# Chunk pairs in the 16-to-32 step of a triangular inverse, and the diagonal blocks of the decay table copied by ScalarE instead of VectorE

## Chip, core and metric

The kernel runs on one core of one Trainium2 chip. The time is device microseconds (us) of that core, the median of several executions. The core's engines each run their own queue in order: TensorE (PE; its weight loads are shown apart as PEld), VectorE (DVE), ScalarE (ACT), GpSimd (POOL), and SyncE (SP), which here issues the DMAs.

## What is computed

One decoder layer on 2048 tokens of width 1024: an input projection; a gated DeltaNet with 8 heads (chunked linear attention); a memory attention with 4 heads beside it; an output projection; layer norm; a squared-ReLU MLP of width 4096; layer norm. All inputs are float32. The part that the change touches is the chunked delta rule. For each chunk of tokens and each head it needs the solution of a unit lower triangular system:

```python
lower = jnp.where(strict, jnp.einsum('bnhcd,bnhsd->bnhcs', k_beta, kc) * decay, 0.0)
a_mat = jnp.eye(CHUNK, dtype=f32) + lower
u = lax.linalg.triangular_solve(a_mat, v_beta, left_side=True, lower=True, unit_diagonal=True)
w = lax.linalg.triangular_solve(a_mat, k_beta * jnp.exp(gc)[..., None], left_side=True,
                                lower=True, unit_diagonal=True)
```

The kernel takes chunks of 128 tokens and forms the inverse of the unit triangular matrix itself, once for each head and chunk.

## The kernel before

**Blocks and stages.** The 2048 tokens go in 4 blocks of 512 (`NB`), a block is 4 chunks of 128 (`NC`). In each block the 8 heads pass through `dense` (the projections aq, ak, av, az, each 24 matmuls with 512 columns, a convolution and a gate), `gdn_a` (key products pkq, the decayed table dl, its inverse by `invert`), and one head later `gdn_b` (the recurrence over the state: products pc and po). Then come the output projection (ao) and the MLP (af). Large products are split into a high and a low fp32r part, so three matmuls make one; the small ones of `invert` and `gdn_b` are plain float32, and the profile counts two passes (a weight load and a matmul each) for one such product.

**The inverse.** `invert` (L803) gets the table L (dl) of a head: 128 rows by 4 chunks by 128 columns. There are 32 inverses in a run, 8 heads by 4 blocks, and each handles 4 chunks at once. It works from small diagonal blocks to large ones:

- The diagonal blocks of 32 rows are copied out of L into Lq, a quad of 32 partitions at a time, with VectorE (L808), and their left halves into LB with GpSimd (L809). From Lq two VectorE instructions pick the 16-row blocks (Lc), and a loop of 15 steps with three VectorE instructions each inverts those 16-row blocks (Xc).
- The step from 16 to 32 rows: Z holds the 16-row inverses at their places, ZT is its transpose by VectorE. XB gets the blocks of Z on its diagonal (ScalarE, four copies, L843). TensorE multiplies LB with the lower half of ZT, one product of 16 columns for each chunk (pq, L849); ScalarE copies the result to Q (L850); TensorE multiplies XB with Q, again one product for each chunk (pp, L853); VectorE subtracts that from ZT (L854). The products use 112 of 128 stationary columns.
- The steps from 32 to 64 (L875 to L891) and from 64 to 128 rows (L893 to L904) have the same shape, but there two chunks share one product: L32, X32, X64 and LP have room for 2 chunk pairs, and a pair occupies different rows and columns. These products are pq and pp with 32 and with 64 columns.

**What sets the order of the work.** All instructions are recorded first. `Recorder.issue` then puts each engine's instructions in one fixed order with a list schedule: it goes by cost formulas for each operation (`Recorder.cost`), latencies between engines (`LAT`, `LAT_FROM`, a margin of 100 ns), and the place in the program as priority. The schedule of the whole kernel is made in one go, so a changed operation in `invert` can move instructions anywhere behind it. TensorE gets the products of `invert`, with matmuls of the projections of other heads between a product and the product that needs its result. Every instruction is issued from one line, so the profile shows L400 for all, and the tile names tell them apart.

Of the kernel before, what the change touches and what calls it, by code (L numbers as in the profile page):

```python
# [10 lines left out]
AF = mybir.ActivationFunctionType  # L11
ALU = mybir.AluOpType
AX = mybir.AxisListType

P = 128
TB = 512
NC = TB // P
# [399 lines left out]
def hybrid_layer(  # L417
# [24 lines left out]
    nc = tc.nc  # L442
# [21 lines left out]
    def small(name, shape, bufs=3, dt=F32):  # L464
        return rec.buf(sm, shape, dt, name, bufs, name)

    def bank(name, tag):
        return rec.buf(ps, (P, TB), F32, tag, PBUFS[tag], name)
# [12 lines left out]
    half = cst.tile([P, 2], F32, name="half")  # L481
# [20 lines left out]
    nc = rec  # L502
# [6 lines left out]
    NI = 1  # L509
    inv = []  # L510
    for i in range(NI):
        d = {}
        for n, shape in (("XB", (NC, P)), ("LB", (NC, P)), ("L32", (2, P)), ("X32", (2, P)), ("X64", (2, P)),
                         ("LP", (2, P)), ("Q", (2 * P,))):
            d[n] = rec.buf(cst, (P,) + shape, F32, n + str(i), 1, n)
            nc.gpsimd.memset(d[n], 0.0)
        inv.append(d)
# [285 lines left out]
    def invert(L, par):  # L803

        Lq = small("Lq", [P, 32, NC], 2)
        for q in range(4):
            r = slice(32 * q, 32 * q + 32)
            nc.vector.tensor_copy(Lq[r].rearrange("p f c -> p c f"), L[r, :, 32 * q:32 * q + 32])  # L808
            nc.gpsimd.tensor_copy(inv[par % NI]["LB"][r, :, 32 * q:32 * q + 16], L[r, :, 32 * q:32 * q + 16])  # L809
        L32, LP = inv[par % NI]["L32"], inv[par % NI]["LP"]  # L810
        for p in range(2):
            rows = slice(64 * p + 32, 64 * p + 64)
# [8 lines left out]
                                       op0=ALU.mult, op1=ALU.add)  # L821
        Xc = small("Xc", [P, 16, NC], 2)
        nc.vector.tensor_copy(Xc, i16.unsqueeze(2).to_broadcast([P, 16, NC]))
        B = small("Bc", [P, 16, NC], 2)
        for j in range(15):
# [3 lines left out]
                                    in1=Lc[:, j:j + 1].to_broadcast([P, w, NC]), op=ALU.mult)  # L829
            nc.vector.tensor_tensor(out=Xc[:, :w], in0=Xc[:, :w], in1=B[:, :w], op=ALU.subtract)  # L830
        Z = small("Z32", [P, NC, 32], 2)
        for hf in range(2):
            nc.vector.tensor_scalar_mul(Z[:, :, 16 * hf:16 * hf + 16], Xc.rearrange("p f c -> p c f"),
                                        half[:, hf:hf + 1])
        ZT = small("ZT32", [P, NC, 32], 2)
        nc.vector.transpose(ZT.rearrange("p c f -> p (c f)"), Z.rearrange("p c f -> p (c f)"))
        XB, LB, X32, X64, Q = (inv[par % NI][n] for n in ("XB", "LB", "X32", "X64", "Q"))
# [1 line left out]
        Y3 = v4(Y)  # L839
        nc.gpsimd.memset(Y, 0.0)  # L840
        quads = [slice(32 * q, 32 * q + 32) for q in range(4)]
        for r in quads:
            nc.scalar.copy(out=XB[r, :, r], in_=Z[r])  # L843

        W = P - 16
        Q16 = Q[:W, :64].rearrange("p (c f) -> p c f", c=NC).part(0)
        pq = bank("pq", "ga%d" % par)[:W, :64].rearrange("p (c f) -> p c f", c=NC)
        for c in range(NC):
            nc.tensor.matmul(pq[:, c], LB[:, c, :W], ZT[:, c, 16:32], start=True, stop=True)  # L849
        nc.scalar.copy(out=Q16, in_=pq)  # L850
        pp = bank("pp", "ga%d" % par)[:W, :64].rearrange("p (c f) -> p c f", c=NC)
        for c in range(NC):
            nc.tensor.matmul(pp[:, c], XB[:, c, :W], Q[:, c * 16:(c + 1) * 16].part(0), start=True, stop=True)  # L853
        nc.vector.tensor_tensor(out=ZT[:W, :, 16:32], in0=ZT[:W, :, 16:32], in1=pp, op=ALU.subtract)  # L854


        ZP = Lq.rearrange("p f c -> p (f c)")[:, :64].rearrange("p (c f) -> p c f", c=2)
        Z = small("Z32", [P, NC, 32], 2)
        for p in range(2):
            odd = slice(64 * p + 32, 64 * p + 64)  # L860
            nc.vector.tensor_copy(ZP[64 * p:64 * p + 32].part(2 * p + 1), ZT[odd, 2:4])
            nc.scalar.copy(out=ZP[odd].part(2 * p), in_=ZT[odd, 0:2])
        nc.vector.transpose(Z.rearrange("p c f -> p (c f)"), ZT.rearrange("p c f -> p (c f)"))
        for p in range(2):
            for u, eng in ((0, nc.gpsimd), (1, nc.vector)):
                q = quads[2 * p + u]
                eng.tensor_copy(X32[q, :, q].part((u, p)), Z[64 * p:64 * p + 32, 2 * u:2 * u + 2])
        for p in range(2):
            for u, eng in ((0, nc.gpsimd), (1, nc.vector)):
                q = quads[2 * u + p]  # L870
# [4 lines left out]
        pq = bank("pq", "ga%d" % par)[:, :64].rearrange("p (c f) -> p c f", c=2)  # L875
# [4 lines left out]
        pp = pb.rearrange("p (c f) -> p c f", c=2)  # L880
# [15 lines left out]
        pq = bank("pq", "ga%d" % par)[:, :P].rearrange("p (c f) -> p c f", c=2)  # L896
# [3 lines left out]
        pp = bank("pp", "ga%d" % par)[:, :P].rearrange("p (c f) -> p c f", c=2)  # L900
# [14 lines left out]
    def gdn_a(h, r, G):  # L915
# [29 lines left out]
        for c0 in range(0, NC, 2):  # L945
# [4 lines left out]
            for c in (c0, c0 + 1):  # L950
                nc.vector.scalar_tensor_tensor(out=dl3[:, c], in0=pkq[:, c - c0, 0], scalar=bh[:, c:c + 1], in1=dl3[:, c],
                                               op0=ALU.mult, op1=ALU.mult)
            nc.vector.tensor_tensor(out=at3[:, c0:c0 + 2], in0=pkq[:, :, 1], in1=at3[:, c0:c0 + 2], op=ALU.mult)
        Y3 = invert(dl3, par)

        pv = trans(v3, "ptv")
# [254 lines left out]
    for b in range(NB):  # L1211
# [14 lines left out]
        r, A = {}, {}  # L1226
# [142 lines left out]
```

## Time and profile before

| what | value |
|---|---|
| median of 3 runs | 2923.58 us (2921.82 to 2924.61) |
| the profiled execution | 2920.42 us |
| its span, first to last instruction | 2918.7 us |
| TensorE busy | 2876.1 us (99%), clock 0.998 |
| VectorE busy | 2181.5 us (75%) |
| ScalarE busy | 1560.7 us (53%) |
| GpSimd busy | 406.1 us (14%) |

The profile is one execution. A row of the timeline gives the start of an instruction or a merged group, its duration, engine, line, operation, output and inputs by tile name, shape, and count; a bracket tells how long the engine was idle before it and what ended that. Matmuls overlap their neighbours, so the time that a matmul takes from TensorE is read from the distance between starts and not from its duration. A row of the groups by line gives busy time, mean duration in ns, idle time before and what ended it.

### The profile page before, as it was taken

Reading aid. Unit: us, or ns where it says so; the run is one execution under the profiler, and the core shown is the slowest. Engines: PE = TensorE matmul, PEld = TensorE weight load, DVE = VectorE, ACT = ScalarE, POOL = GpSimd, SP = SyncE. Lnnn points to the kernel's source line nnn. Section 1 sums busy time; section 2 is a strip of 40 time slices with the busy share of each in tenths; the row PEclk is TensorE's granted clock in tenths of the full one; section 3 lists DMA queues with packets and bytes.
Section 4 is the critical chain, followed back from the end, with each engine's and each line's share of the span. In section 5 each row is a group of like instructions: output and inputs, shape, how many; then the busy total and the mean of one; then the engine's idle time right before and its main releaser. Section 6 shows DMA issues by size and latency. Waiting matters only on the chain.

```text
span 2918.7 us, 43334 instructions
## 1 busy us (share of the span) xinstructions
PE 2876.1 (99%) x14660; PEld 2407.3 (82%) x14660; DVE 2181.5 (75%) x5792; ACT 1560.7 (53%) x3774; POOL 406.1 (14%) x1029
## 2 busy tenths in 40 slices
PE   8999999999999999999999999999999999999998
PEld 6888778888788888888888888888888888888886
DVE  7998987666788886666678887756667888676667
ACT  6677635444366663555446665344454667444443
POOL 2233101000132211000022321100002222010000
PEclk9999999999999999999999999999999999999999
DMA  7655567555743322444473332244447332324444
GB/s 282 245 202 199 185 225 242 189 193 185 277 156 130 127 87 80 159 141 136 150 273 141 132 116 99 87 151 145 148 165 257 137 139 86 103 94 150 147 145 137
DMA packets 127710, 469.83 MB, mean 161 GB/s; under 512 B 14464, under 2 KB 16896, under 8 KB 109056
## 3 DMA queue, kind: packets, MB, share of 16 engines
q1 hardware_dynamic: 126912, 467.00, 46.9%
q8 instruction: 116, 1.90, 0.3%
q14 instruction: 106, 0.87, 0.1%
q10 hardware_dynamic: 576, 0.06, 0.0%
HBM read 402.97 MB, written 64.03 MB: 160 GB/s over the span
## 4 chain that ended last, share of the span: by engine, by line
PE 88%; DVE 6%; ACT 3%; DMA 1%; POOL 1%; issue 1%; POOLq 0%; SPq 0%; DVEq 0%; ACTq 0%
PE af L400 43%; PE ao L400 8%; PE aq L400 6%; PE az L400 5%; PE av L400 5%; PE ak L400 5%; PE amq L400 3%; PE pc L400 3%; PE pq L400 2%; PE po L400 1%; DVE y L400 1%; PE pkq L400 1%; PE pp L400 1%; PE pmo L400 1%; PE sps L400 1%
## 5 line engine op out<-in xcount | busy, mean ns | idle before, releaser
L400 DVE TENSOR_TENSOR whl<-wraw,whl 128x1024 fp32r<-128x1024 f32 (+1 forms) x446 | 541.6, 1218 | 414.6 <-ACT whl L400 412.9
L400 PE MATMUL af<-Thi,whl 128*128 128x512 f32 (+1 forms) x2304 | 649.1, 366 | 6.4 <-DVE whl L400 6.4
L400 ACT CAST whl<-wraw 128x1024 fp32r<-128x1024 f32 (+1 forms) x446 | 467.2, 1047 | 345.0 <-PE af L400 241.2
L400 PEld LDWEIGHTS af<-Thi,whl 128*128 128x128 f32 x2304 | 416.2, 189 | 77.5 <-DVE whl L400 7.3
L400 PE MATMUL af<-whl,xh 128*128 128x512 f32 x1536 | 472.1, 390 | 0.5 <-ACT whl L400 0.4
L400 PE MATMUL af<-Tlo,whl 128*128 128x512 f32 (+1 forms) x1152 | 421.3, 366 | 0.0
L400 PE MATMUL af<-whl,xl 128*128 128x512 f32 x896 | 345.5, 389 | 0.0
L400 PEld LDWEIGHTS af<-whl,xh 128*128 128x128 f32 x1536 | 287.9, 188 | 62.9 <-DVE whl L400 1.5
L400 PE MATMUL ao<-whl,ch 128*128 128x512 f32 x768 | 252.4, 402 | 0.3 <-DVE y L400 0.2
L400 PEld LDWEIGHTS af<-Tlo,whl 128*128 128x128 f32 x1152 | 217.2, 189 | 34.7
L400 POOL TENSOR_SCALAR ve<-mv 128x1 f32<-128x1 f32 x34 | 25.8, 760 | 1466.0 <-DVE mv L400 1439.0
L400 ACT ACTIVATE rl<-af 128x512 f32<-128x512 f32 x128 | 76.5, 597 | 274.4 <-PE af L400 272.6
L400 PEld LDWEIGHTS af<-whl,xl 128*128 128x128 f32 x896 | 168.2, 188 | 35.1
L400 PE MATMUL aq<-Thi,whl 128*128 128x512 f32 x512 | 181.9, 413 | 7.0 <-ACT Thi L400 7.0
L400 PE MATMUL av<-Thi,whl 128*128 128x512 f32 x512 | 178.3, 406 | 0.1
L400 PE MATMUL ak<-Thi,whl 128*128 128x512 f32 x512 | 174.0, 400 | 0.0
L400 DVE SCALAR_TENSOR_TENSOR y<-y,af 128x512 f32<-128x512 f32 x224 | 146.5, 680 | 35.4 <-PE af L400 35.4
L400 PE MATMUL az<-Thi,whl 128*128 128x512 f32 x512 | 171.3, 399 | 1.5 <-DVE whl L400 1.5
L400 PEld LDWEIGHTS ao<-whl,ch 128*128 128x128 f32 x768 | 141.6, 188 | 27.1 <-DVE y L400 0.9
L400 PE MATMUL ao<-whl,cl 128*128 128x512 f32 x384 | 154.2, 404 | 0.0
L400 PEld LDWEIGHTS aq<-Thi,whl 128*128 128x128 f32 x512 | 95.4, 192 | 21.8 <-ACT Thi L400 7.0
L400 PEld LDWEIGHTS az<-Thi,whl 128*128 128x128 f32 x512 | 95.0, 188 | 18.7 <-DVE whl L400 1.9
(256 smaller groups left out, 5839.6 us busy)
## 6 DMA issues: line engine op xcount, KB each, us to landing
wraw<-in_w_ff_dram SPq DMA_DIRECT2D x224, 512.0 KB, 4.2
whl<-wsc SPq DMA_DIRECT2D x108, 1024.0 KB, 4.8
wraw<-tsc SPq DMA_DIRECT2D x128, 512.0 KB, 3.3
wsc<-whl SPq DMA_DIRECT2D x36, 1024.0 KB, 6.0
wraw<-in_w_out_dram SPq DMA_DIRECT2D x48, 512.0 KB, 3.7
wraw<-in_w_in_dram SPq DMA_DIRECT2D x35, 512.0 KB, 7.0
wq<-in_w_ff_dram SPq DMA_DIRECT2D x64, 256.0 KB, 4.3
tsc<-wq SPq DMA_DIRECT2D x64, 256.0 KB, 3.3
```

The source lines that it names most:

```text
L400: o.fn(*[res(a) for a in o.args], **{k: res(v) for k, v in o.kw.items()})
```

## The change

In the step from 16 to 32 rows, two chunks (c and c + 2) now share one product. LB holds two chunks side by side in each 32-row block, so it is (2, 128) in place of (4, 128), and so is XB. The product of LB with the halves of ZT of both chunks gives for every row both the wanted 16 columns and those of the other chunk; two ScalarE activations copy it to Q, each with a per-partition scale (`half`, 1 on one 16-row half of each quad and 0 on the other), which makes the unwanted part zero. XB has to hold the 16-row inverses of two chunks on its diagonal: a VectorE shuffle (Xr) exchanges the 16-row halves of chunks 2 and 3, and a VectorE multiply-add (Xp) merges them with chunks 0 and 1. The four ScalarE copies to XB take half as many elements. Both products are now made 2 times with 32 columns in place of 4 times with 16, and the first one has 128 stationary columns in place of 112. Apart from that, the four copies of the diagonal blocks into Lq go from VectorE to ScalarE.

```diff
-        for n, shape in (("XB", (NC, P)), ("LB", (NC, P)), ("L32", (2, P)), ("X32", (2, P)), ("X64", (2, P)),
+        for n, shape in (("XB", (2, P)), ("LB", (2, P)), ("L32", (2, P)), ("X32", (2, P)), ("X64", (2, P)),
...
-            nc.vector.tensor_copy(Lq[r].rearrange("p f c -> p c f"), L[r, :, 32 * q:32 * q + 32])
-            nc.gpsimd.tensor_copy(inv[par % NI]["LB"][r, :, 32 * q:32 * q + 16], L[r, :, 32 * q:32 * q + 16])
+            nc.scalar.copy(out=Lq[r].rearrange("p f c -> p c f"), in_=L[r, :, 32 * q:32 * q + 32])
+            nc.gpsimd.tensor_copy(inv[par % NI]["LB"][r, :, r].rearrange("p u (k f) -> p u k f", k=2),
+                                  L[r, :, 32 * q:32 * q + 16].rearrange("p (k u) f -> p u k f", k=2))
...
+        Xr = small("Xr", [P, 16, 2], 1)
+        nc.vector.stream_shuffle(Xr, Xc[:, :, 2:4], list(range(16, 32)) + list(range(16)))
+        Xp = small("Xp", [P, 2, 16], 1)
+        nc.vector.scalar_tensor_tensor(out=Xp, in0=Xr.rearrange("p f c -> p c f"), scalar=half[:, 1:2],
+                                       in1=Z[:, 0:2, 0:16], op0=ALU.mult, op1=ALU.add)
...
-        for r in quads:
-            nc.scalar.copy(out=XB[r, :, r], in_=Z[r])
+        for q, r in enumerate(quads):
+            nc.scalar.copy(out=XB[r, :, 32 * q:32 * q + 16], in_=Xp[r])
+        pq = bank("pq", "ga%d" % par)[:, :64].rearrange("p (u f) -> p u f", u=2)
+        for c in range(2):
+            nc.tensor.matmul(pq[:, c], LB[:, c], ZT[:, c:NC:2, 16:32], start=True, stop=True)
+        Q16 = Q[:, :64].rearrange("p (u f) -> p u f", u=2)
+        nc.scalar.activation(Q16[:, :, 0:16].part(0), pq[:, :, 0:16], AF.Copy, scale=half[:, 0:1])
+        nc.scalar.activation(Q16[:, :, 16:32].part(3), pq[:, :, 16:32], AF.Copy, scale=half[:, 1:2])
         W = P - 16
-        Q16 = Q[:W, :64].rearrange("p (c f) -> p c f", c=NC).part(0)
-        pq = bank("pq", "ga%d" % par)[:W, :64].rearrange("p (c f) -> p c f", c=NC)
-        for c in range(NC):
-            nc.tensor.matmul(pq[:, c], LB[:, c, :W], ZT[:, c, 16:32], start=True, stop=True)
-        nc.scalar.copy(out=Q16, in_=pq)
-        pp = bank("pp", "ga%d" % par)[:W, :64].rearrange("p (c f) -> p c f", c=NC)
-        for c in range(NC):
-            nc.tensor.matmul(pp[:, c], XB[:, c, :W], Q[:, c * 16:(c + 1) * 16].part(0), start=True, stop=True)
-        nc.vector.tensor_tensor(out=ZT[:W, :, 16:32], in0=ZT[:W, :, 16:32], in1=pp, op=ALU.subtract)
+        pp = bank("pp", "ga%d" % par)[:W, :64]
+        for c in range(2):
+            nc.tensor.matmul(pp[:, c * 32:(c + 1) * 32], XB[:, c, :W], Q[:, c * 32:(c + 1) * 32].part(0, 3),
+                             start=True, stop=True)
+        zt = ZT[:W].rearrange("p (k u) f -> p u k f", k=2)[:, :, :, 16:32]
+        nc.vector.tensor_tensor(out=zt, in0=zt, in1=pp.rearrange("p (u k f) -> p u k f", u=2, k=2), op=ALU.subtract)
```

Because the whole schedule is made anew, the order changes in many places. Three of them follow; a row is line, operation, output and inputs by tile name, shape of the streamed operand or the result, and count.

On TensorE, the first inverse of block 0, with the key projection (ak) of another head around it. Before:

```order
L400 MATMUL pq<-ZT_1239,LB 112x16 x4
L400 MATMUL pkq<-kq 128x256 x6
L400 MATMUL pp<-Q,XB 112x16 x4
L400 MATMUL ak<-Thi,whl 128x512 x2
L400 MATMUL ak<-Tlo,whl 128x512
L400 MATMUL ak<-Thi,whl 128x512 x2
```

And now:

```order
L400 MATMUL pq<-ZT_1242,LB 128x32 x2
L400 MATMUL ak<-Thi,whl 128x512
L400 MATMUL pkq<-kq 128x256 x6
L400 MATMUL pp<-Q,XB 112x32 x2
L400 MATMUL ak<-Thi,whl 128x512
L400 MATMUL ak<-Tlo,whl 128x512
L400 MATMUL ak<-Thi,whl 128x512 x2
```

Each product of the step stands 2 times in place of 4, and between the two products there is one ak matmul more.

On TensorE, the last inverse of block 1 (the 16th of the run), its step from 64 to 128 rows, beside the output projection (ao) and the transposes of the memory attention (pmT). Before:

```order
L400 MATMUL pq<-YP,LP 128x64 x2
L400 MATMUL ao<-whl,cl 128x512
L400 MATMUL pmT<-ident,pr 128x128 x2
L400 MATMUL ao<-whl,ch 128x512 x2
L400 MATMUL ao<-whl,cl 128x512
L400 MATMUL pmT<-ident,pr 128x128
L400 MATMUL pp<-Q,X_150 128x64 x2
```

And now:

```order
L400 MATMUL ao<-whl,cl 128x512
L400 MATMUL ao<-whl,ch 128x512 x2
L400 MATMUL ao<-whl,cl 128x512
L400 MATMUL pq<-YP,LP 128x64 x2
L400 MATMUL pp<-Q,X_149 128x64 x2
L400 MATMUL ao<-whl,ch 128x512 x2
```

The product pp, which needs the ScalarE copy of pq, now follows pq directly; in the last inverses of blocks 2 and 3 it is the same.

On ScalarE, the first inverse of block 0, from the copies to XB on. Before:

```order
L400 COPY XB<-Z_1226 32x4x32 x4
L400 COPY Q<-pq 112x64
L400 COPY Lq<-ZT_1239 32x64 x2
L400 COPY Y<-ZT_1239 32x4x32 x4
L400 COPY Q<-pq 128x64
L400 COPY raw<-ak 128x512
```

And now:

```order
L400 COPY XB<-Xp 32x2x16 x4
L400 ACTIVATE Q<-pq,half 128x2x16 x2
L400 COPY Lq<-ZT_1242 32x64 x2
L400 COPY Y<-ZT_1242 32x4x32 x4
L400 COPY Q<-pq 128x64
L400 COPY Lq<-dl 32x4x32 x4
L400 ACTIVATE Y<-pp 32x2x32 x2
```

Two activations stand where one copy to Q stood, and the four Lq copies of the next head's inverse have come in between the copy of pq to Q and the instructions that read pp; the copy out of the bank of ak (raw) has moved behind them.

## The prediction

> **What bounds the kernel now.** I read the page first: busy times by engine, and the chain of work that ended last.
>
> ```profile
> span 2918.7 us, 43334 instructions
> PE 2876.1 (99%) x14660; PEld 2407.3 (82%) x14660; DVE 2181.5 (75%) x5792; ACT 1560.7 (53%) x3774; POOL 406.1 (14%) x1029
> PE 88%; DVE 6%; ACT 3%; DMA 1%; POOL 1%; issue 1%; POOLq 0%; SPq 0%; DVEq 0%; ACTq 0%
> ```
>
> TensorE works in 2876.1 of 2918.7 us, so all its idle time is 42.6 us, and 88% of the last chain is its own. The changed work lies in the stages of the heads, so I cut those out next: first the heads of block 0, then those of blocks 1 to 3, in windows of 292 us (columns: PE, PEld, DVE, ACT, POOL busy, clock, DMA share, GB/s).
>
> ```profile
> 73.00:365.00 292.00, 286.51 (x1612) 240.64 (x1610) 268.28 (x1005) 203.38 (x634) 87.55 (x209) 1.00 0.57 208
> ```
>
> ```profile
> 803.00:1095.00 292.00, 290.13 (x1650) 245.16 (x1649) 242.19 (x994) 185.37 (x635) 72.44 (x219) 1.00 0.35 125
> 1533.00:1825.00 292.00, 290.13 (x1651) 245.19 (x1651) 239.89 (x974) 181.35 (x627) 68.91 (x208) 1.00 0.34 121
> 2263.00:2555.00 292.00, 290.38 (x1645) 245.14 (x1644) 234.94 (x917) 178.41 (x604) 61.42 (x180) 1.00 0.33 115
> ```
>
> In these stages too TensorE is the limit: it idles 5.5 us in block 0 and 1.9, 1.9 and 1.6 us in the others. VectorE has 24 us left in block 0 and about 50 us elsewhere, ScalarE 89 us and more. So the time should follow the work of TensorE as long as the others deliver in time. The last view is the timeline of TensorE at the first inverse:
>
> ```profile
> 103.03 0.87 PE L400 MATMUL pq<-ZT,LB 128*112 128x16 f32 x8
> 103.75 0.96 PE L400 MATMUL pkq<-kq 128*128 128x256 f32 x6
> 104.55 0.86 PE L400 MATMUL pp<-Q,XB 128*112 128x16 f32 x8
> 105.26 0.70 PE L400 MATMUL ak<-Thi,whl 128*128 128x512 f32 x2
> 105.80 0.40 PE L400 MATMUL ak<-Tlo,whl 128*128 128x512 f32 x1
> ...
> 107.41 0.53 PE L400 MATMUL pq<-Lq,L 128*128 128x32 f32 x4
> 107.77 0.48 PE L400 MATMUL ak<-Thi,whl 128*128 128x512 f32 x1
> 108.09 0.39 PE L400 MATMUL av<-Thi,whl 128*128 128x512 f32 x1
> 108.32 0.40 PE L400 MATMUL av<-Tlo,whl 128*128 128x512 f32 x1
> 108.55 0.40 PE L400 MATMUL av<-Thi,whl 128*128 128x512 f32 x1
> ```
>
> A matmul of 512 columns in a stream takes 0.23 us from start to start (108.09, 108.32, 108.55). The eight passes of pp start at 104.55 and the next matmul at 105.26, so 0.71 us; but the two ak behind them take 0.54 us where two such take 0.45. The group therefore costs 0.71 + 0.09 = 0.80 us, 0.100 for each pass. The four passes of pq with Lq and L, whose form is that of the changed product (128 stationary columns, 32 streamed), cost 0.36 + (0.32 - 0.23) = 0.45 us, 0.113 each.
>
> **The change part by part. TensorE.** The first product has 0.72 us to the next start, and the pkq behind it takes 0.80 us where 0.72 is usual:
>
> ```profile
> 807.40 0.88 PE L400 MATMUL pkq<-kq 128*128 128x256 f32 x6
> 808.12 0.40 PE L400 MATMUL av<-Thi,whl 128*128 128x512 f32 x1
> ```
>
> So it also costs 0.80 us, and the step 1.60 us in each inverse. Now pq has four passes of a form that is in the trace, 0.45 us. The four passes of pp keep 112 stationary columns and stream 32 in place of 16: no row shows that form. Its lower bound is 4 x 0.100 = 0.40 us, its upper bound the 0.45 of the 128-column form. I take 0.40, since streamed columns do not seem to count below 128, as the products of the recurrence show:
>
> ```profile
> 814.95 0.38 PE L400 MATMUL pc<-state,ck 128*128 128x128 f32 x2
> 815.16 0.39 PE L400 MATMUL po<-state,qd 128*128 128x128 f32 x2
> 815.31 0.48 PE L400 MATMUL aq<-Thi,whl 128*128 128x512 f32 x1
> 815.62 0.40 PE L400 MATMUL aq<-Tlo,whl 128*128 128x512 f32 x1
> ```
>
> Four passes with 128 streamed columns take 0.36 + (0.31 - 0.23) = 0.44 us, no more than the four with 32. The step is then 0.85 us (up to 0.90), and an inverse saves 0.75 us (at least 0.70). All 32 inverses lie in stages where TensorE is the limit: 32 x 0.75 = 24.0 us, at least 22.4.
>
> [...]
>
> **ScalarE and VectorE.** The rows of the groups by line that carry the costs (busy us, mean ns, idle before):
>
> ```profile
> L400 DVE COPY Lq<-dl 32x128 f32<-32x128 f32 x128 | 35.0, 274 | 2.0
> L400 DVE STREAM_SHUFFLE Bc<-Xc 128x32 f32<-128x32 f32 x32 | 6.0, 187 | 0.2
> L400 DVE SCALAR_TENSOR_TENSOR gp<-gp,gz 128x32 f32<-128x32 f32 x28 | 5.1, 183 | 0.0
> L400 DVE SCALAR_TENSOR_TENSOR Lc<-Lq,half,Lc 128x64 f32<-128x64 f32 x32 | 8.9, 277 | 0.2
> ```
>
> ```profile
> L400 ACT COPY XB<-Z 32x128 f32<-32x128 f32 x128 | 37.8, 295 | 15.1 <-DVE Z L400 13.8
> L400 ACT COPY Lq<-ZT 32x64 f32<-32x64 f32 x64 | 15.5, 243 | 21.5 <-DVE ZT L400 20.8
> L400 ACT ACTIVATE vb<-ptv,vbs 128x128 f32<-128x128 f32 x128 | 36.7, 367 | 11.6 <-PE ptv L400 11.6
> L400 ACT COPY vt<-pc 128x128 f32<-128x128 f32 x128 | 34.4, 269 | 88.1 <-PE pc L400 87.1
> L400 ACT COPY Q<-pq 112x64 f32<-112x64 f32 x32 | 6.6, 208 | 8.5 <-PE pq L400 8.1
> ```
>
> For each inverse VectorE loses 4 copies of 274 ns (1.10 us) and gains a shuffle (187 ns) and a multiply-add over 32 elements, which lies between 183 and 277 ns; I take 230. That is 0.68 us less, 5.4 us in a block of 8 heads.
>
> ScalarE gains four Lq copies. Their form is that of the XB copies, 295 ns, so 1.18 us. The four XB copies shrink from 128 to 32 elements: from 295 at 128 and 243 at 64, I estimate 217 at 32, 0.31 us less. The copy to Q (208 ns) becomes two activations with a per-partition scale. Such a scale costs about 98 ns (367 against 269), and 32 elements in place of 64 save about 28 (from 269 at 128 and 208 at 64), so 0.28 us each and 0.35 us more. ScalarE has 1.22 us more for each inverse, 9.8 us in a block: 70 to 73% in block 0, 62 to 66% elsewhere. Neither engine becomes the limit, and both sums lie beside TensorE's work. What hides them is the stream of projection matmuls; without it each inverse would pay the 1.22 us.
>
> The four LB copies of GpSimd keep their number and their elements, in three dimensions: no row shows that, but GpSimd is at 21 to 30% in these stages, and by the code the copies can be made a whole loop of VectorE ahead of their product. The shuffle and the multiply-add lengthen the way from Xc to pp by up to 0.42 us, the waits for ScalarE's Lq that from dl to Lc by a few tenths; other heads' matmuls cover both, as far as the new order provides.
>
> **New waits.** A product that reads Q has to wait for ScalarE. How long, this place shows, where TensorE did wait:
>
> ```profile
> 2512.66 0.55 PE L400 MATMUL pq<-YP,LP 128*128 128x64 f32 x4
> 2513.02 0.47 PE L400 MATMUL ao<-whl,cl 128*128 128x512 f32 x1
> 2513.24 0.27 ACT L400 COPY Q<-pq 128x128 f32<-128x128 f32 x1 [0.92 <-PE pq L400]
> 2513.65 0.63 PE L400 MATMUL pp<-Q,X 128*128 128x64 f32 x4 [0.16 <-ACT Q L400]
> ```
>
> From the slot behind pq (2513.02) it takes 0.22 us to ScalarE's start, 0.27 for the copy, 0.14 to pp: 0.63 us. With two activations it is 0.22 + 0.56 + 0.14 = 0.92 us. The new order puts one ak and six pkq between pq and pp at the first inverse, 0.23 + 0.72 = 0.95 us, and counted over all 32 inverses nowhere less. So that wait should just be covered. The second place in the order is not covered: in the last inverses of blocks 1 to 3, pp follows pq at once and TensorE idles 0.63 us, 1.9 us in all.
>
> **The sum.** The profiled execution is 2920.42 us: 2920.4 - 24.0 + 1.9 = 2898.3. The median of the runs lies 3.2 us above that execution, and I expect the same of the changed kernel: 2901.5 us.
>
> **Rivals.** First, the new order eats part of the gain. The order was made from cost formulas, and the ScalarE copies come into the way of others at places like the third one, where four of them (1.18 us) stand between Q and the readers of pp. If the idle time of the four stages doubles (5.5 + 1.9 + 1.9 + 1.6 = 10.9 us), the saving is 24.0 - 1.9 - 10.9 = 11.2 us, so 2912.4. For it speaks block 0, where VectorE has only 24 us left; against it the relief of VectorE there.
>
> Second, slower: ScalarE holds up TensorE. The Lq copies wait in ScalarE's queue for dl, and behind them stand the copies out of the PSUM banks that TensorE needs back. If the four copies' 1.18 us fell on TensorE in every inverse, the loss would be 37.8 us against 24.0 gained, so 2937.4; from 0.75 us for each inverse it turns the result. Against it: ScalarE idles a third of these stages, and TensorE waits for it little now, as the list of waits shows (total us, times, longest):
>
> ```profile
> PE pq L400 <- DVE YP L400: 2.4, 10, 0.5
> PE pc L400 <- ACT vt L400: 1.8, 5, 0.5
> ```
>
> Third, no difference: a pass costs by what it streams, and the step streams 16 passes x 16 = 8 x 32 = 256 columns before and after. Then nothing is saved but the 1.9 us of new waits are paid, 2925.5. The rows of pc and po speak against it. [...]
>
> **The numbers.** The forecast (a saving of 16 to 29 us) gets 0.64, the partial gain 0.18, slower 0.09, no difference 0.09. The low end, 2895, is the forecast with 24.0 us saved, no new wait, and block 0's idle of 5.5 us nearly gone through VectorE's relief; the high end, 2914, takes in most of the partial gain. About 0.2% (5.8 us) is what a measurement of this kernel can tell from no change. Faster by more than that holds the forecast and nearly all of the partial gain, 0.81; within it 0.11; slower 0.08.
>
> **What would show it.** The page after should have 256 fewer passes and about 24 us less TensorE time, spans of the four head stages shorter by about 6 us each, groups pq with ZT at 0.45 us and pp with XB at 0.40 to 0.45 us by starts, a wait of pp for Q of about 0.6 us at the end of blocks 1 to 3, ScalarE up by some 39 us and VectorE down by some 22 us. I am wrong if TensorE's idle time grows by more than 10 us, and the waits will then name ScalarE's Q, Lq or Y, or a PSUM bank that ScalarE gave back late.

## The result and the profile after

| | before | after |
|---|---|---|
| median of 4 runs | 2924.01 us (2921.82 to 2924.61) | 2906.32 us (2903.26 to 2907.78) |
| the profiled execution | 2920.42 us, clock 0.998 | 2907.78 us, clock 0.995 |

The ratio is 0.9939, with a 95% interval of 0.9922 to 0.9957. The change takes 17.7 us off the median; 22.1 were forecast, and 2906.3 lies inside the range. The profiled execution of the kernel before was faster than all four of its runs and that of the kernel after the slowest of its four, so the two show only 12.6 us of this. First the page of the kernel after: span, busy time of the engines, and the chain that ended last by engine.

```profile
span 2906.1 us, 42964 instructions
PE 2862.3 (98%) x14404; PEld 2384.7 (82%) x14404; DVE 2165.3 (75%) x5760; ACT 1607.6 (55%) x3934; POOL 416.3 (14%) x1029
PE 82%; DVE 8%; ACT 6%; issue 1%; POOL 1%; DMA 1%; SPq 0%; POOLq 0%; ACTq 0%; DVEq 0%
```

TensorE has the 256 passes fewer. ScalarE gained 46.9 us (39 were forecast), VectorE lost 16.2 (22). TensorE's part of the chain fell from 88 to 82%, and VectorE and ScalarE took over what it lost: the end now hangs on them more often. The same windows of the head stages as before the change, in the kernel after:

```profile
73.00:365.00 292.00, 286.66 (x1560) 238.13 (x1558) 264.46 (x1003) 213.40 (x673) 84.24 (x211) 0.99 0.59 210
803.00:1095.00 292.00, 289.33 (x1604) 241.87 (x1603) 241.91 (x989) 198.30 (x673) 76.98 (x213) 0.99 0.35 124
1533.00:1825.00 292.00, 289.36 (x1594) 241.40 (x1594) 237.39 (x946) 189.65 (x643) 73.66 (x201) 0.99 0.35 122
2263.00:2555.00 292.00, 289.38 (x1596) 241.11 (x1595) 233.88 (x883) 182.72 (x620) 67.60 (x174) 1.00 0.33 115
```

TensorE now idles 5.3, 2.7, 2.6 and 2.6 us in them, against 5.5, 1.9, 1.9 and 1.6. The column of the clock has fallen to 0.99 in three of the four; it was 1.00 in all. The first inverse on TensorE, in the timeline of the kernel after:

```profile
104.04 0.53 PE L400 MATMUL pq<-ZT,LB 128*128 128x32 f32 x4
104.40 0.48 PE L400 MATMUL ak<-Thi,whl 128*128 128x512 f32 x1
104.72 0.87 PE L400 MATMUL pkq<-kq 128*128 128x256 f32 x6
105.42 0.49 PE L400 MATMUL pp<-Q,XB 128*112 128x32 f32 x4
105.75 0.48 PE L400 MATMUL ak<-Thi,whl 128*128 128x512 f32 x1
106.06 0.39 PE L400 MATMUL ak<-Tlo,whl 128*128 128x512 f32 x1
```

By starts pq costs 0.36 + (0.32 - 0.23) = 0.45 us, and pp 0.33 + (0.31 - 0.23) = 0.41. Over all 32 inverses the medians are 0.454 and 0.414; before it was 0.806 for either. The step went from 1.61 to 0.87 us, and 32 x 0.74 = 23.7 us of passes are gone, as forecast.

So where are the missing microseconds? The waits of TensorE in the kernel after (total us, times, longest) name the first of them:

```profile
PE pq L400 <- DVE YP L400: 3.0, 8, 0.5
PE ao L400 <- DVE y L400: 2.7, 4, 0.8
PE pp L400 <- ACT Q L400: 1.8, 4, 0.4
```

The wait for Q is the one that the prediction put at 1.9 us. The wait of ao for y is new: it was 0.2 us in all. Three of the four waits of either of the last two rows stand at the last inverses of blocks 1 to 3. This is block 1 in the timeline of the kernel after:

```profile
1074.49 0.60 PE L400 MATMUL pq<-YP,LP 128*128 128x64 f32 x4
1075.05 1.21 DVE L400 TENSOR_TENSOR whl<-wraw,whl 128x1024 fp32r<-128x1024 f32 x1
1075.13 0.27 ACT L400 COPY Q<-pq 128x128 f32<-128x128 f32 x1 [0.75 <-PE pq L400]
...
1075.54 0.63 PE L400 MATMUL pp<-Q,X 128*128 128x64 f32 x4 [0.45 <-ACT Q L400]
...
1076.25 0.68 DVE L400 SCALAR_TENSOR_TENSOR y<-y,ao 128x512 f32<-128x512 f32 x1
...
1076.98 0.98 PE L400 MATMUL ao<-whl,ch 128*128 128x512 f32 x2 [0.82 <-DVE y L400]
```

TensorE first waits 0.45 us for Q. The ao behind pp needs an accumulator that VectorE empties with the addition to y, and in VectorE's queue a weight split of 1.21 us stands ahead of that addition. So 0.82 us follow. What comes next shows in the windows of 2 us around that place, kernel after (the column behind the five engines is the clock):

```profile
1074.00:1076.00 2.00, 1.55 (x11) 1.21 (x9) 1.94 (x4) 0.62 (x3) 0.00 (x0) 1.00 0.02 4
1076.00:1078.00 2.00, 1.18 (x6) 0.75 (x6) 1.80 (x5) 1.62 (x6) 0.00 (x0) 0.82 0.38 45
1078.00:1080.00 2.00, 2.00 (x9) 1.81 (x8) 1.96 (x6) 1.20 (x5) 0.00 (x0) 0.50 0.92 250
1080.00:1082.00 2.00, 2.00 (x11) 1.61 (x10) 0.13 (x1) 0.27 (x2) 0.00 (x0) 0.82 0.58 229
1082.00:1084.00 2.00, 2.00 (x17) 1.75 (x15) 1.14 (x3) 0.59 (x1) 0.00 (x0) 1.00 0.00 0
```

Behind the two gaps the granted clock is 0.50 for a while, and TensorE, although busy, gets through less: 9 and 11 matmuls in a window, against 17 in the next (of mixed sizes). The loss is 2 x (0.18 + 0.50 + 0.18) = 1.7 us, more than the two gaps together. The same happens behind the last inverse of block 2 (0.50 from 1790.68 us on) and behind gaps of 1.45 and 0.43 us in block 0 (0.50 from 340.01 us on); behind the same two gaps of block 3 it doesn't (1.00 from 2498 to 2506 us). Summed over windows of 2 us between 52 us and the last 24 us, the low clock costs 5.2 us; before the change the same sum is 0.0. In the start-up ahead of 52 us it is 3.4 against 1.7. These figures belong to the two profiled executions (clock 0.998 and 0.995) and not to the medians: the mean granted clock is 0.9965 over the four runs of the kernel after, and 0.9965 too over the 21 runs of the kernel before that stand beside e1.

From one profiled execution to the other this makes -23.7 for the passes, +5.2 and +1.7 for the clock, and +1.2 for idle time of TensorE as a whole (43.8 us against 42.6). The sum is -15.6, and -12.6 was measured: 3 us more were lost that aren't attributed. Some of it may be in waits of weight loads, whose matmuls still count as work: that of ptv for Y grew from 1.7 to 7.4 us, for one, and the whole list from 82.8 to 94.4. Between the medians the clock takes nothing, so there the 6.0 us lost against the 23.7 are left to idle time and such waits. By blocks, from the first aq to the first af, the head stages became 2.4, 2.7, 2.7 and 3.8 us shorter, where about 6 each was forecast; the block without a low clock gained most.

### The profile page after: what moved, and what is told of

It reads as the page before. It is cut to its first block, busy times and chain, and to the rows that moved or that the text cites. A ratio compares the mean times of both kernels' runs of the same rounds, so it can differ in the third digit from the quotient of the medians.

```text
span 2906.1 us, 42964 instructions
## 1 busy us (share of the span) xinstructions
PE 2862.3 (98%) x14404; PEld 2384.7 (82%) x14404; DVE 2165.3 (75%) x5760; ACT 1607.6 (55%) x3934; POOL 416.3 (14%) x1029
## 3 DMA queue, kind: packets, MB, share of 16 engines
q1 hardware_dynamic: 126912, 467.00, 46.9%
## 4 chain that ended last, share of the span: by engine, by line
PE 82%; DVE 8%; ACT 6%; issue 1%; POOL 1%; DMA 1%; SPq 0%; POOLq 0%; ACTq 0%; DVEq 0%
PE af L400 44%; PE ao L400 8%; PE aq L400 6%; PE az L400 4%; PE ak L400 3%; PE av L400 3%; PE amq L400 2%; PE pc L400 2%; PE po L400 1%; DVE y L400 1%; PE pkq L400 1%; DVE whl L400 1%; PE pq L400 1%; PE pmo L400 1%; ACT Lq L400 1%
## 5 line engine op out<-in xcount | busy, mean ns | idle before, releaser
L400 PE MATMUL az<-Thi,whl 128*128 128x512 f32 x512 | 177.9, 405 | 1.5 <-DVE whl L400 1.5
```

Source lines behind the costliest of these rows:

```text
L400: o.fn(*[res(a) for a in o.args], **{k: res(v) for k, v in o.kw.items()})
```

## The experiments

The pass term came out; the time is 4.8 us above the forecast. The first theory is that the removed passes set the time and that the order of the new schedule gave some of it back in gaps and low clock. Its rival is that ScalarE's added work, the Lq copies above all, costs the rest. Each experiment was timed in 5 rounds; e1 to e4, e5 to e8 and e9 to e12 share their runs of the kernel before (medians 2924.2, 2924.8 and 2924.5 us). In the table, "clock" is what the low clock costs and "idle" is TensorE's idle time, both of the profiled execution between 52 us and the last 24 us.

| kernel | median us | ratio to before (95%) | clock us | idle us |
|---|---|---|---|---|
| before | 2924.0 | | 0.0 | 19.6 |
| after | 2906.3 | 0.9939 (0.9922 to 0.9957) | 5.2 | 20.8 |
| e1_pair_only | 2899.5 | 0.9919 (0.9905 to 0.9932) | 5.1 | 20.8 |
| e2_lq_only | 2927.9 | 1.0016 (1.0007 to 1.0025) | 5.2 | 22.1 |
| e3_double_passes | 2912.3 | 0.9962 (0.9950 to 0.9975) | 0.0 | 14.1 |
| e4_margin80 | 2916.5 | 0.9976 (0.9967 to 0.9985) | 8.5 | 28.5 |
| e5_swap | 2904.6 | 0.9934 (0.9921 to 0.9946) | 5.1 | 20.2 |
| e6_order_of_e3 | 2907.4 | 0.9944 (0.9931 to 0.9956) | 0.0 | 21.4 |
| e7_after_actcost | 2915.7 | 0.9966 (0.9953 to 0.9978) | 17.1 | 28.6 |
| e8_before_actcost | 2927.4 | 1.0011 (1.0002 to 1.0021) | 3.4 | 21.4 |
| e9_pair_only_m80 | 2916.7 | 0.9975 (0.9966 to 0.9984) | 10.3 | 28.6 |
| e10_before_m80 | 2925.2 | 1.0002 (0.9994 to 1.0011) | 6.9 | 20.9 |
| e11_pair_only_actcost | 2916.6 | 0.9973 (0.9963 to 0.9984) | 15.4 | 32.8 |
| e12_lq_pool | 2899.0 | 0.9916 (0.9902 to 0.9929) | 1.7 | 18.5 |

### The two parts apart: e1_pair_only and e2_lq_only

The pairs without the move of the Lq copies, made from the kernel after:

```diff
-            nc.scalar.copy(out=Lq[r].rearrange("p f c -> p c f"), in_=L[r, :, 32 * q:32 * q + 32])
+            nc.vector.tensor_copy(Lq[r].rearrange("p f c -> p c f"), L[r, :, 32 * q:32 * q + 32])
```

> The chunk pairs as in the change, but the four Lq copies stay on VectorE. Theory A (TensorE's passes set the time; of the 24 us that they save, some 6 us are lost where the new order leaves TensorE idle at the end of a block, and to the lower clock right behind that): the order of this kernel has between 0.9 and 1.4 us of matmuls between the last pq and pp of every block, so no such idle time; about 2900 us, clock 0.998 in every run. Theory B (the 6 us are ScalarE's added 1.2 us for each inverse, which delay copies that TensorE waits for): three fourths of that are gone, also about 2901 us. Alone it does not tell them apart; it gives the worth of the pairs without the move.

The move alone, made from the kernel before by the opposite edit:

```diff
-            nc.vector.tensor_copy(Lq[r].rearrange("p f c -> p c f"), L[r, :, 32 * q:32 * q + 32])
+            nc.scalar.copy(out=Lq[r].rearrange("p f c -> p c f"), in_=L[r, :, 32 * q:32 * q + 32])
```

> Only the move of the four Lq copies to ScalarE, the products as before. Theory A: no pass is saved and the order has no product behind its producer at the block ends, so the time of the kernel before, 2924 us, within 4. Theory B: ScalarE is later and nothing is gained, 2928 to 2931 us.

The pairs alone give 2899.5 us, 24.7 less than before and 6.8 less than the whole change. The move alone costs 3.7 us. Both expectations for e1 gave its time, but the clock of 0.998 that the first one wanted in every run is 0.996 in all four; the 2927.9 us of e2 lie on the border between its two. Taken by themselves these two speak for the rival: the pairs are worth all of the forecast 24, and the move takes part of it away. Rows of the groups by line, of the kernel after, give the move its price:

```profile
L400 ACT COPY Lq<-dl 32x128 f32<-32x128 f32 x128 | 53.3, 417 | 2.8 <-DVE dl L400 1.3
L400 ACT COPY XB<-Xp 32x32 f32<-32x32 f32 x128 | 27.3, 213 | 15.4 <-DVE Xp L400 14.1
L400 ACT ACTIVATE Q<-pq,half 128x32 f32<-128x32 f32 x64 | 15.3, 285 | 3.4 <-PE pq L400 3.2
```

An Lq copy takes 417 ns on ScalarE, where the prediction put 295. TensorE's idle time and low clock are the same in the profiles of e1 and of the kernel after, 20.8 and 5.1 or 5.2 us. Its weight loads do wait more in the kernel after, 94.4 us in all against 82.6, and some of that is for ScalarE. The longest growth of a row, from e1:

```profile
PEld pq L400 <- ACT YP L400: 2.3, 4, 0.6
```

And from the kernel after:

```profile
PEld pq L400 <- ACT YP L400: 6.7, 13, 0.9
```

Whether that comes from the added work or from another order these two runs can't say. The next ones had to tell a price from an accident of the order.

### The passes taken back: e3_double_passes and e6_order_of_e3

In the first, every product of the step is issued twice, so that the step has 16 passes again; the results are the same.

```diff
             nc.tensor.matmul(pq[:, c], LB[:, c], ZT[:, c:NC:2, 16:32], start=True, stop=True)
+            nc.tensor.matmul(pq[:, c], LB[:, c], ZT[:, c:NC:2, 16:32], start=True, stop=True)
...
             nc.tensor.matmul(pp[:, c * 32:(c + 1) * 32], XB[:, c, :W], Q[:, c * 32:(c + 1) * 32].part(0, 3),
                              start=True, stop=True)
+            nc.tensor.matmul(pp[:, c * 32:(c + 1) * 32], XB[:, c, :W], Q[:, c * 32:(c + 1) * 32].part(0, 3),
+                             start=True, stop=True)
```

> The changed kernel with each product of the step from 16 to 32 rows issued twice, the second overwriting the first with the same values: 8 more passes for each inverse, 0.85 us. Theory A: 27 us more TensorE work than the changed kernel (2906.3), less the block-end idle time that this order does not have (5 us): 2926 to 2929 us. Theory B: 27 us more and nothing back, 2933 us. If passes did not count (streamed columns or waits set the time), it stays below 2912.

The schedule of e3 is a new one. So the second, shown here against e3, lets the planner count the doubled products, and leaves them out when the instructions are emitted. All engines then have the order of e3, without its 256 passes.

```diff
+        o.ghost = kw.pop("ghost", False)
...
+                if o.ghost:
+                    continue
...
-            nc.tensor.matmul(pq[:, c], LB[:, c], ZT[:, c:NC:2, 16:32], start=True, stop=True)
+            nc.tensor.matmul(pq[:, c], LB[:, c], ZT[:, c:NC:2, 16:32], start=True, stop=True, ghost=True)
...
-                             start=True, stop=True)
+                             start=True, stop=True, ghost=True)
```

> The changed kernel in the order of the kernel with doubled products: the planner counts each product of the step twice, but only one of each is issued. So the order is that of the run at 2912.3 us, which lost the least time beside the passes, and the passes are those of the changed kernel. If the passes set the time and the order the rest, 27 us less: 2885 us. If the doubled passes were only a cover for waits on ScalarE and VectorE that come out again without them: 2895 to 2905 us.

The theories went wrong in both; the 2912.3 us of e3 lie at the edge of its last case, in which something other than the passes sets the time. The page of e3 has as many passes as the kernel before and nearly its busy time, and yet the kernel is 11.9 us faster than before:

```profile
span 2909.0 us, 43540 instructions
PE 2871.1 (99%) x14660; PEld 2407.5 (83%) x14660; DVE 2169.0 (75%) x5760; ACT 1609.2 (55%) x3934; POOL 411.7 (14%) x1029
```

Of the 11.9 us, 5.5 are idle time of TensorE (14.1 against 19.6), and an estimated 4 are clock (mean 0.9978 over the runs of e3, 0.9965 over those of the kernel before); the rest isn't attributed. By starts the doubled products cost their full price, 0.90 us for pq and 0.80 for pp. Without them e6 should be 32 x 0.85 = 27 us faster than e3 if the passes set the time. It is 4.9 us faster (2912.3 to 2907.4):

```profile
span 2904.1 us, 43028 instructions
PE 2859.6 (98%) x14404; PEld 2380.5 (82%) x14404; DVE 2168.1 (75%) x5760; ACT 1606.5 (55%) x3934; POOL 409.3 (14%) x1029
```

Between 52 us and the last 24 us the clock is at fault in neither (0.0 us each); in the start-up e6 has 3.4 us of low clock and e3 1.7. TensorE's idle time takes 7 of the missing 22 us (14.1 to 21.4). More of it shows where the weight loads wait; these are waits of e3:

```profile
PEld pq L400 <- issue: 3.7, 12, 0.6
...
PEld pp L400 <- ACT Q L400: 1.6, 6, 0.4
...
PEld pq L400 <- ACT Lq L400: 0.2, 1, 0.2
```

And these of e6:

```profile
PEld pq L403 <- issue: 11.5, 31, 1.0
...
PEld pp L403 <- ACT Q L403: 6.4, 12, 0.8
...
PEld pq L403 <- ACT Lq L403: 3.3, 5, 1.1
PEld pkq L403 <- DVE at L403: 2.3, 3, 0.8
```

The passes had covered the way of an inverse from engine to engine. Once they are out, with everything else in its place, TensorE comes to the next product earlier and finds Q or Lq not ready. ("issue" means that the profile doesn't show what ended the wait.) The whole list of weight-load waits sums to 71.3 us in e3 and 98.8 in e6. Such a wait costs time even where the matmuls show no gap. The second inverse of e6:

```profile
141.18 0.47 PEld L403 LDWEIGHTS pp<-Q,XB 128*112 128x112 f32 x4 [0.28 <-ACT Q L403]
141.19 0.57 PE L403 MATMUL pp<-Q,XB 128*112 128x32 f32 x4
141.60 0.71 PE L403 MATMUL av<-Thi,whl 128*128 128x512 f32 x2
```

The load waits 0.28 us for Q, the matmul behind it not at all by the profile; and yet from pp to the next start it is 0.41 us, where the same place in the kernel after has 0.32. The simple form of the first theory, that the passes set the time whatever the order, is refuted. But e6's order was planned with the passes in it, so its 4.9 us are their worth in that order and not in one planned without them.

### Other orders of the same work: e4_margin80, e9_pair_only_m80, e10_before_m80

One constant of the planner is changed, in the kernel after, in e1 and in the kernel before.

```diff
-MARGIN = 100
+MARGIN = 80
```

> The changed kernel with the planner's margin at 80 in place of 100 ns: the same instructions in another order, in which the last pq and pp of each block have 0.7 to 0.9 us of matmuls between them. Theory A: the idle time at the block ends and the clock dips behind it go, 2899 to 2903 us and clock 0.998 in every run. Theory B: ScalarE has as much to do as in the changed kernel, 2905 to 2908 us.

> The pairs with the Lq copies on VectorE, at the planner's margin of 80 ns: beside the whole change at that margin (2916.5 us). If the move to ScalarE costs time in itself (6.8 us at margin 100), this is some 5 to 7 us faster than that, 2909 to 2912 us. If the 6.8 us are an accident of one order, the two may stand either way within 10 us.

> The kernel before at margin 80: with the run above and the whole change at that margin it gives the worth of the passes in another family of orders. If the passes are worth their TensorE time in any order, it is 24 us above the pairs alone, 2933 to 2936 us; if orders scatter by 10 us, 2922 to 2936.

The expectation for e4 missed by some 14 us. Its head stages did become shorter, 379.3 to 379.6 us in blocks 1 to 3 (before 384, after 380 to 382). But the first row of TensorE's waits in e4 shows what came behind them, where the MLPs of the blocks begin:

```profile
PE af L400 <- DVE whl L400: 11.8, 4, 3.0
```

This wait is 4.7 us in the kernel after, so 7 us were lost there, and the low clock costs more (8.5 us in the table, 5.2 in the kernel after). With this constant e1's kernel is no faster than the whole change (2916.7 and 2916.5), so the move of Lq costs nothing here. The kernel before hardly notices (2925.2).

### Another planner cost: e7_after_actcost, e8_before_actcost, e11_pair_only_actcost

The planner takes each ScalarE instruction out of SBUF for 100 ns longer; again in the kernels after, before and e1.

```diff
-            return 52 + 0.833 * n + (0 if psum else 42) + 93 * len(scal) + ((305 if scal else 198) if "accum_out" in kw else 0)
+            return 52 + 0.833 * n + (0 if psum else 142) + 93 * len(scal) + ((305 if scal else 198) if "accum_out" in kw else 0)
```

> The changed kernel with the planner's cost of a ScalarE instruction that reads SBUF raised by 100 ns (42 to 142), as the trace has it (four Lq copies take 1.2 us where the planner counts 0.8). A planner that knows ScalarE's times should leave fewer waits for it: 2898 to 2904 us. If the loss against the 24 us is not ScalarE's, no gain beyond a shuffled order: 2902 to 2912 us.

> The kernel before with the same planner cost: the partner of the run above. If the passes are worth 24 us in any order, the two lie 24 us apart, give or take the idle time of each order (10 us); this one alone 2915 to 2928 us.

> The pairs with the Lq copies on VectorE, at the raised ScalarE cost: beside the whole change with it (2915.7 us) and the kernel before with it (2927.4 us). If the move costs time in itself: 2909 to 2911 us. If the passes are worth 24 us: 2903 us. If the order decides: anything between 2900 and 2918.

The planner now has the Lq copies nearer to their 417 ns (the 1.2 us of the expectation is the prediction's price; four copies take 1.67), and the kernel is 9.4 us slower than after, beyond both ranges of its expectation. The whole change and the pairs alone are again level (2915.7 and 2916.6). The nine kernels of these three settings make one table, in us:

| planner | before | pairs only | whole change | worth of the pairs | price of the Lq move |
|---|---|---|---|---|---|
| as it was | 2924.2 | 2899.5 | 2906.3 | 24.7 | 6.8 |
| margin 80 | 2925.2 | 2916.7 | 2916.5 | 8.5 | -0.2 |
| ScalarE cost + 100 | 2927.4 | 2916.6 | 2915.7 | 10.8 | -0.9 |

In all three orders the pairs gain, from 8.5 to 24.7 us for the same passes removed; the 24 us in any order, which the expectations of e8, e10 and e11 held possible, did not come. Some of the spread is clock: its mean over the runs is 0.9937 and 0.9931 for the pairs alone in the last two rows (e9, e11) against 0.9954 and 0.9961 for the kernel before (e10, e8), an estimated 5 and 9 us; with the planner as it was it is some 1.5 us (0.9960 against 0.9965). The move has a price in one order of three.

### The Lq copies on GpSimd: e12_lq_pool

```diff
-            nc.scalar.copy(out=Lq[r].rearrange("p f c -> p c f"), in_=L[r, :, 32 * q:32 * q + 32])
+            nc.gpsimd.tensor_copy(Lq[r].rearrange("p f c -> p c f"), L[r, :, 32 * q:32 * q + 32])
```

> The change with the four Lq copies on GpSimd in place of ScalarE or VectorE. If ScalarE's 1.2 us more for each inverse are what cost the 6.8 us, this is as fast as with the copies on VectorE, 2897 to 2901 us, or faster for VectorE's relief. If any move off VectorE costs (a longer way from dl to Lc, another order), 2904 to 2912 us.

With 2899.0 us it is level with e1, although the copies are slower still, as the groups by line of e12 show:

```profile
L400 POOL COPY Lq<-dl 32x128 f32<-32x128 f32 x128 | 59.5, 465 | 50.5 <-DVE dl L400 46.2
```

With the planner as it was, the copies cost something only on ScalarE, which is what the rival says. With the two other orders they cost nothing there. I take the 6.8 us for a property of this order; that ScalarE's work as such costs time isn't shown, and not excluded for the one order. The two versions e1 and e12 beat both kernels, by 24.7 and 25.5 us against before.

### The gap at the ends of the blocks: e5_swap

Three weight splits of VectorE, those ahead of the y addition at the ends of blocks 1 to 3, are moved behind it. Nothing else changes its place.

```diff
+        pes = sorted((o for o in out if o.eng == "PE"), key=lambda o: (o.start, o.i))
+        dves = sorted((o for o in out if o.eng == "DVE"), key=lambda o: (o.start, o.i))
+        for u, v in zip(pes, pes[1:]):
+            if "LP" in tag(u) and "X64" in tag(v):
+                n = next(n for n, o in enumerate(dves) if o.start > u.start and {"y", "ao"} <= tag(o))
+                s = next(dves[m] for m in range(n - 1, n - 4, -1) if tag(dves[m]) == {"wraw", "whl"})
...
+                s.start = dves[n].start + 0.001
```

> The changed kernel with three instructions moved: at the ends of blocks 1 to 3, VectorE's weight split (whl) that stood ahead of the addition to y goes behind it; everything else in the same order. In the changed kernel TensorE idles there 0.45 us for Q and then 0.82 us for that addition, and in the profile the granted clock is low for some 4 us behind it in blocks 1 and 2 (about 1.7 us lost each). If the idle time starts the low clock, and the second wait goes: 3 x 0.8 = 2.5 us less idle time and up to 3 x 1.7 us less by the clock, 2900 to 2904 us, against 2906.3. If the low clock comes from something else: 2904 us with the clock as before. If the split, now 0.85 us later, is what TensorE waits for next, nothing is gained: 2906 us.

The wait of ao for y is gone, but two matmuls on, the same split is ahead of the half of Y that VectorE writes, and a new wait stands there. From the list of e5's waits:

```profile
PE ptv L410 <- DVE Y L410: 2.2, 3, 0.7
```

So 2.5 us of waiting became 2.2. The median of 2904.6 us (2904.1 to 2906.0) is 1.7 below the kernel after, whose runs reach from 2903.3 to 2907.8: not to be told from no change. What the swap did tell is about the clock. The windows of 2 us of e5, at the ends of blocks 1 and 2:

```profile
1076.00:1078.00 2.00, 1.26 (x8) 0.84 (x8) 1.97 (x4) 1.51 (x6) 0.00 (x0) 1.00 0.01 4
1078.00:1080.00 2.00, 2.00 (x13) 1.48 (x11) 1.97 (x5) 1.14 (x4) 0.00 (x0) 1.00 0.70 201
...
1788.00:1790.00 2.00, 1.27 (x8) 1.22 (x8) 1.97 (x5) 1.10 (x5) 0.00 (x0) 0.77 0.26 57
1790.00:1792.00 2.00, 2.00 (x7) 1.52 (x6) 1.39 (x4) 0.81 (x4) 0.00 (x0) 0.50 0.84 246
```

The same gaps, 0.45 + 0.74 us, are followed by a full clock in block 1 and by 0.50 in block 2 (more on this in the last section).

## Why the prediction came out as it did

- **The passes: right.** A step of 0.87 us (0.85 forecast), 23.7 us of passes gone (24.0). The pp of 112 stationary and 32 streamed columns costs 0.41 us, or 0.104 for a pass, where a pass with 16 streamed columns cost 0.101 (0.806 us for 8); so its price goes by passes and hardly by what they stream. The rival of the streamed columns is refuted.
- **The new wait for Q: right.** At the three places where it was looked for, pp starts 1.05 us behind pq (1074.49 to 1075.54 in block 1), 0.60 more than the 0.45 us of four such passes, for 0.63 forecast; the profile counts 0.45 us of it as idle time. The wait stands once more in block 0, which wasn't foreseen, so that the 1.8 us of the list, for four waits, come near the forecast 1.9 for three by luck. Elsewhere the two activations (285 ns each, 280 forecast) stay covered.
- **ScalarE's work: mis-sized.** XB (213 ns for 217) was right. Lq wasn't: 417 ns for 295. The price came from the XB copy, which has as many elements but writes runs of 32 in a row, while Lq is written with a stride ("p f c -> p c f"). That the stride makes the difference is argued, not tested. The 122 ns are 15.6 us more over 128 copies; the net for each inverse is some 1.6 us and not 1.22. The two new VectorE instructions came as forecast, with medians of 186 ns (Xr, 187 forecast) and 242 ns (Xp, 230).
- **The rivals.** The saving of 17.7 us lies between the 22.1 forecast and the 11.2 of the partial gain, but not by that rival's sum: TensorE's idle time in the four stages rose by 2.4 us and not by 10.9. The low clock, which no rival had, added 5.2 us between the two profiled executions and nothing between the medians. What the runs show in its place is the Lq copies on ScalarE: with them on VectorE or GpSimd (e1, e12) the same planner gives 6.8 and 7.3 us less. ScalarE holding up TensorE in every inverse didn't occur; its waits in the kernel after are the few above.
- **The median against the profile: wrong.** The prediction put the median 3.2 us above the profiled execution, as before the change. It lies 1.5 us below, for the profile of before was taken at a clock of 0.998 and that of after at 0.995.
- **The step that failed** is "All 32 inverses lie in stages where TensorE is the limit: 32 x 0.75 = 24.0 us". The 24 us are TensorE's work, but how much of them the time gives back is set by the order, by its waits and by the low clock behind them: 4.9 of 27 us in e6 against e3, 8.5 and 10.8 in two other orders, 24.7 in e1. A busy share of 99% had been read as a limit; a part of that share is matmuls whose weight loads wait for the inverse, as the row of pp in e6 shows. That the whole change landed near the sum is in part the luck of the order that came with it.
- **Left open:** which instruction of the order holds TensorE up in the slower settings. From one profiled execution to the other, low clock and idle time together rise by 11.0 us for 8.5 us of time from the kernel after to e4, by 19.7 for 8.3 to e7, by 13.0 for 17.6 from e1 to e9 and by 22.3 for 18.1 from e1 to e11. So gaps and the low clock behind them are a large part of what an order costs, but the sums don't come out one by one.

## What to carry to other kernels

Price a removed instruction by the distances between starts, but credit it to the time only after runs without it: here that gave 4.9 of 27 us in an order planned with it, and from 8.5 to 24.7 us, for the same 24 us of passes, in orders planned without it. In a kernel whose whole order is planned in one go, compare an edit under two or three settings of the planner before it is praised or blamed; the settings moved the time by up to 17 us, as much as the edit. Price a copy from a row with the same layout at its output, not only the same number of elements: here the row with as many elements had 295 ns, and the copy took 417.

## What the runs showed of the hardware

TensorE's granted clock fell to 0.50 behind short gaps: 0.45 + 0.82 us of idle time within 2.5 us (kernel after, block 1). It stayed there for 3.413 us by the trace, in blocks 0, 1 and 2 alike, which costs an estimated 1.7 us each time (half of 3.41). A longer gap need not do it, as the windows of the kernel before show at the start of the first MLP, where TensorE waits 2.96 us:

```profile
429.00:431.00 2.00, 2.00 (x16) 1.78 (x14) 2.00 (x5) 0.79 (x2) 0.00 (x0) 1.00 0.02 4
431.00:433.00 2.00, 0.69 (x5) 0.31 (x3) 2.00 (x5) 0.87 (x2) 0.00 (x0) 1.00 0.04 8
433.00:435.00 2.00, 0.36 (x3) 0.36 (x4) 2.00 (x4) 0.00 (x0) 0.20 (x1) 1.00 0.00 0
```

Where the gaps fall seems to make a difference. In the profiled execution of the kernel after the low clock starts at 340.01, 1077.29 and 1790.68 us; these starts are 737.28 and 713.39 us apart, which is 216 and 209 times 3.413. Cut at this pace, the stretches around the last inverses of blocks 1 and 3 of the kernel after are:

```profile
1073.88:1077.29 3.41, 2.15 (x13) 1.64 (x12) 3.14 (x7) 1.65 (x7) 0.00 (x0) 1.00 0.01 2
1077.29:1080.71 3.42, 3.42 (x12) 2.79 (x11) 2.80 (x7) 1.92 (x7) 0.00 (x0) 0.50 0.85 207
...
2497.24:2500.65 3.41, 2.96 (x18) 2.36 (x16) 2.94 (x8) 1.75 (x5) 0.00 (x0) 1.00 0.00 0
2500.65:2504.07 3.42, 2.60 (x16) 2.02 (x15) 3.19 (x8) 2.83 (x10) 0.00 (x0) 1.00 0.50 153
```

In block 1 both gaps fall into one stretch, TensorE is busy for 2.15 of 3.41 us (63%), and the next stretch has half the clock. In block 3 they are divided between two stretches, busy for 2.96 and 2.60 us, and the clock stays. The gap of 2.96 us of the kernel before is divided too, if that execution is cut at the same pace from its own low clock at 43.94 us:

```profile
429.65:433.06 3.41, 2.04 (x15) 1.55 (x13) 3.41 (x7) 1.11 (x2) 0.00 (x0) 1.00 0.03 7
433.06:436.48 3.42, 1.84 (x15) 1.84 (x16) 3.42 (x6) 0.00 (x0) 1.60 (x2) 1.00 0.24 57
```

Counted over these two profiled executions, between 52 us and the last 24 us, the low clock follows the one stretch at full clock in which TensorE is busy for less than half (1.53 of 3.41 us, ahead of 340.01 us in the kernel after), 2 of 11 with 50 to 70%, and none of 1645 with more. The two are busy for 63%, and the clock stayed behind stretches with 60 and 54%, those of the gap of 2.96 us. So the busy share of one such stretch doesn't settle it alone; what else the clock goes by, no run here shows.
